# One step of a hybrid attention encoder on one core: GpSimd products in pieces, the first token loads, and the place of the per-layer inputs

## The chip, the cores and the metric

The kernel runs on one core of one Trainium2 chip, as one launch. The metric is device time in microseconds (us) of that launch. A core has five engines with queues of their own: TensorE (PE in the profile; its weight loads are shown apart as PEld), VectorE (DVE), ScalarE (ACT), GpSimd (POOL) and SyncE (SP), which issues all DMAs of this kernel in one order.

## The reference, cut to what matters

One layer over 2,048 prompt tokens and 32 sample tokens, width 1,024, all in float32. The parts that the change touches are the first norm and projection, the splits of every matrix product, and the per-layer inputs `p`.

```python
def rmsnorm(x, g, eps=EPS):
    y = x * lax.rsqrt(jnp.mean(x * x, axis=-1, keepdims=True) + eps)
    return y * g

z  = rmsnorm(hp, g_attn) @ w_in            # q, k, v of group A (4 heads, two maps) and group B (8 heads)
oa = diff_attn(qa, ka, va, t5_table, lam)  # softmax(map 1) - lam * softmax(map 2), chunk-causal
ob = band_attn(qb, kb, vb, band_table)     # each 64-token chunk sees itself and the 8 before
h  = hp + concat(rmsnorm(oa) * 0.8, rmsnorm(ob)) @ w_out
c  = rmsnorm(h, g_mlp)
h  = h + square(relu(c @ w_up)) @ w_down   # 1024 -> 4096 -> 1024
h  = h + sigmoid(h @ w_ple_gate) * (p @ w_ple_proj)      # p: 256 wide per token
y  = rmsnorm(h, g_final)
```

The keys and values of both groups are outputs too. The sample tokens attend to 128 cached keys besides their own.

## The kernel before

**Splitting.** TensorE works on a rounded 32-bit type (`F32R`). To keep float32 accuracy each operand is held as a high and a low half, and every product is three matmuls (`mm3`, L164 to L170: high by high at L168, high by low at L169, low by high at L170). The low half is "raw minus high". `split` (L146) makes both: the high half by a copy on ScalarE (L149) or VectorE (L151), the low half by a subtraction (L153) on GpSimd or VectorE. `wunit` (L155) loads a weight tile of 128 x 1,024 (`wr`, two buffers), and has it split on ScalarE and GpSimd into `wh` and `wl` (three buffers each). So each weight tile takes one GpSimd instruction of 1,024 columns.

**Stages.** `run` (L1074) writes the program in this order: constants and gains (`consts`); the norm and transpose of token blocks 0 and 1 (`prep`, four tiles of 128 tokens a block); the group A projections of these blocks (`proj`); the lambda, the relative biases and the per-layer inputs (`lam`, `biases`, `prep_p`); group A attention of the first half (`attn_a`), around which the scheduler lays the group B projections of blocks 0 to 2 and the norms of blocks 2 and 3; the cached keys and values (`caches`); the group B projection of block 3; group B attention (`attn_b`); then output projections, MLP (`mlp`), gate (`gate`) and final norm (`final`), laid around the rest of the attention. A block is 512 tokens; block 3 carries the 32 sample tokens as well.

**Who decides the order.** The tile framework takes the program order as a priority, and a scheduler that simulates the engines fixes, when the kernel is built, the order of the instructions on each engine. On the chip each engine runs its own list strictly in order, and so does SyncE with the DMAs. A tile name has a fixed number of buffers, handed out in program order: a later tile of the same tag can't be written before an earlier one has its buffer and has given it back.

**PSUM.** Two banks are tag `mm` (projections, MLP and most others), three are `s` (attention scores), two `tp` (attention transposes), one `o` (attention outputs).

**`prep`** (L297), for each tile: load `x`; square it on ScalarE with a row sum; `rsqrt` (L172) turns the sum `st` into the row factor, by Ln and Exp on ScalarE (L177, L178) and one Newton step in four small instructions (L179 to L182), on VectorE here; the factor is transposed and broadcast through PSUM (`rp`, `rb`); the tokens are transposed on TensorE (`xp`, L319), stored as `xT`, scaled on VectorE (L323) into `a32`, and split into `aH` (VectorE, L151) and `aL` (GpSimd). The PSUM tiles of the first two blocks come from the three banks `s`.

**`prep_p`** (L753): per block a load `pn`, eight transposes a block through PSUM tag `tp` (`ppt`), a split on ScalarE and VectorE into the tags `qh` and `ql` (two buffers each, shared with the projections), and the stores `pS`, which only `gate` reads, much later.

**`biases`** (L227) builds one row per head and spreads it to 128 rows in DRAM (`dba`, `dbb`); `attn_a` reads the table `ba` from it.

Of the kernel before, what the change touches and what calls it, by code (L numbers as in the profile page):

```python
# [76 lines left out]
JB = [(0, 1), (2, 3), (4, 5), (6, 7, 8)]  # L77
ONP = (28, 1, 6)
ONQ = (8, 1, 1)


def drain(gen):
    for _ in gen:
        pass
# [48 lines left out]
class Kern:  # L133
# [5 lines left out]
    def dma(self, dst, src):  # L139
# [3 lines left out]
            src = src.bitcast(F32)  # L143
        self.nc.sync.dma_start(dst, src)

    def split(self, hi, lo, raw, hi_eng="act", lo_eng="pool"):  # L146
        nc = self.nc
        if hi_eng == "act":
            nc.scalar.activation(hi, raw, AF.Copy)  # L149
        else:  # L150
            nc.vector.tensor_copy(hi, raw)  # L151
        eng = nc.gpsimd if lo_eng == "pool" else nc.vector
        eng.tensor_tensor(lo, raw, hi.bitcast(F32), op=ALU.subtract)  # L153

    def wunit(self, src, shape, hi_eng="act", lo_eng="pool"):  # L155
        nc = self.nc
# [15 lines left out]
    def rsqrt(self, pool, src, n, scale, eps, eng, tag="rs", np_=P, bufs=None):  # L172
        nc = self.nc
        v = pool.tile([P, n], F32, tag=tag + "v", bufs=bufs, name="rsv")[:np_]
        nc.scalar.activation(v, src, AF.Copy, scale=scale, bias=eps)
        y0 = pool.tile([P, n], F32, tag=tag + "y", bufs=bufs, name="rsy")[:np_]
        nc.scalar.activation(y0, v, AF.Ln)  # L177
        nc.scalar.activation(y0, y0, AF.Exp, scale=-0.5)  # L178
        eng.tensor_tensor(v, v, y0, op=ALU.mult)  # L179
        eng.tensor_tensor(v, v, y0, op=ALU.mult)  # L180
        eng.tensor_scalar(v, v, -0.5, 1.5, op0=ALU.mult, op1=ALU.add)
        eng.tensor_tensor(y0, y0, v, op=ALU.mult)  # L182
        return y0
# [7 lines left out]
    def consts(self, cp):  # L191
        nc, a = self.nc, self.a
        self.ident = cp.tile([P, P], F32, name="ident")
        make_identity(nc, self.ident)
        ones = cp.tile([P, P], F32, name="ones")
        nc.gpsimd.memset(ones, 1.0)
        self.ones = cp.tile([P, P], F32R, name="ones_r")
        nc.vector.tensor_copy(self.ones, ones)

        def cols(name, ap, k):  # L200
            t = cp.tile([P, k], F32, name=name)
            self.dma(t, ap.rearrange("(k p) -> p k", p=P))
            return t

        self.g_attn = cols("g_attn_s", a["g_attn"][0], 8)
        self.g_mlp = cols("g_mlp_s", a["g_mlp"][0], 8)
        self.g_b = cols("g_b_s", a["out_norm_b"][0], 4)
        self.g_sub = cols("g_sub_s", a["subln_g"][0], 1)
        nc.vector.tensor_scalar(self.g_sub, self.g_sub, 1.0 - LAM_INIT, None, op0=ALU.mult)
# [84 lines left out]
    def actpair(self):  # L294
        return [self.act.tile([P, 8, BLK], F32R, tag="act", name=n) for n in ("aH", "aL")]

    def prep(self, b, acts, pp, mm, tag):  # L297
        nc = self.nc
        aH, aL = acts[b]
        for c0, n in toks(b):  # L300
            t0 = 512 * b + c0
            x = pp.tile([P, D], F32, tag="x", name="x")
            self.dma(x[:n], self.xsrc(t0, n))
            a32 = pp.tile([P, 8, P], F32, tag="a32", name="a32")
            st = pp.tile([P, 1], F32, tag="st", name="st")
            nc.scalar.activation(
                a32[:n].rearrange("p a b -> p (a b)"), x[:n], AF.Square, accum_out=st[:n]
            )
            r = self.rsqrt(pp, st[:n], 1, 1.0 / D, EPS, nc.vector, "r1", n)
            rp = mm.tile([P, 512], F32, tag=tag, name="rp")  # L310
            nc.tensor.transpose(rp[:, :n], r.broadcast_to([n, P]), self.ident[:n, :n])
            rb = pp.tile([P, P], F32, tag="rb", name="rb")
            nc.scalar.activation(rb[:, :n], rp[:, :n], AF.Copy)
            xt = pp.tile([P, 8, P], F32, tag="xt", name="xt")
            for h in range(2):
                xp = mm.tile([P, 4, P], F32, tag=tag, name="xp")
                for k in range(4):
                    kk = 4 * h + k
                    nc.tensor.transpose(xp[:, k, :n], x[:n, kk * P : kk * P + P], self.ident[:n, :n])  # L319
                nc.scalar.activation(xt[:, 4 * h : 4 * h + 4, :n], xp[:, :, :n], AF.Copy)  # L320
                for k in range(4):
                    kk = 4 * h + k
                    nc.vector.scalar_tensor_tensor(  # L323
                        a32[:, kk, :n], xp[:, k, :n], self.g_attn[:, kk : kk + 1], rb[:, :n],
                        op0=ALU.mult, op1=ALU.mult,
                    )
            self.dma(self.xT[:, :, t0 : t0 + n], xt[:, :, :n])
            self.split(aH[:, :, c0 : c0 + n], aL[:, :, c0 : c0 + n], a32[:, :, :n], "dve", "pool")
            yield

    def ktok(self, b):
# [421 lines left out]
    def prep_p(self, sg, wk, ps):  # L753
        nc, a = self.nc, self.a
        for b in range(4):
            t0 = 512 * b
            n = BN[b]
            pn = wk.tile([P, 5, DPLE], F32, tag="pn", bufs=2, name="pn")
            self.dma(pn[:, :4], a["p_prompt"][0, 0, t0 : t0 + 512].rearrange("(i p) c -> p i c", p=P))
            if b == 3:  # L760
                self.dma(pn[:SS, 4], a["p_sample"][0, 0])
            for k in range(2):
                hi = sg.tile([P, BLK], F32R, tag="qh", bufs=2, name="pph")
                lo = sg.tile([P, BLK], F32R, tag="ql", bufs=2, name="ppl")
                pieces = [(0, 512)] + ([(512, SS)] if b == 3 else [])
                for c0, w in pieces:
                    tp = ps.tile([P, 512], F32, tag="tp", name="ppt")
                    for i in range(max(w // P, 1)):
                        m = min(w, P)
                        nc.tensor.transpose(  # L770
                            tp[:, P * i : P * i + m], pn[:m, c0 // P + i, P * k : P * k + P], self.ident[:m, :m]
                        )
# [12 lines left out]
    def onorm(self, b, wk, ps, tag, dst):  # L785
        nc = self.nc
        n, t0 = BN[b], 512 * b
        sq = wk.tile([P, BLK], F32, tag="acc", bufs=2, name="sqacc")[:, :n]
        for k in range(4, 8):
            raw = self.raw_o(wk, k, t0, n)  # L790
            if k == 4:
                nc.scalar.activation(sq, raw, AF.Square)
            else:
                nc.scalar.activation(raw, raw, AF.Square)
                nc.gpsimd.tensor_tensor(sq, sq, raw, op=ALU.add)
        yield from self.colnorm2(sq, b, 1.0 / 512, wk, ps, tag, dst, [])

    def oload(self, b, wk, up, out):
# [20 lines left out]
    def outproj(self, b, wk, oact, ps, acc):  # L819
# [5 lines left out]
        for d in range(8):  # L825
# [13 lines left out]
            if d == 0:  # L839
                nc.scalar.activation(sq, h, AF.Square)  # L840
            else:
                tmp = wk.tile([P, BLK], F32, tag="tmp", bufs=4, name="tmp")[:, :n]
                nc.scalar.activation(tmp, h, AF.Square)
                nc.gpsimd.tensor_tensor(sq, sq, tmp, op=ALU.add)
            self.dma(self.hS[:, d, t0 : t0 + n], h)
            yield

# [118 lines left out]
    def gate(self, b, h, up, act, md):  # L966
# [11 lines left out]
        for dq in range(2):  # L978
# [3 lines left out]
            for d4 in range(4):  # L982
                d = 4 * dq + d4
                wh, wl = self.wunit(Wg[:, P * d : P * d + P].rearrange("(k p) c -> p k c", p=P), [8, P])
                for s0, sn in SUBS[b]:
# [8 lines left out]
                    nc.vector.tensor_scalar(sm, pg, 0.0, None, op0=ALU.min)  # L994
                    nc.scalar.activation(sg, sg, AF.Exp, scale=-1.0)
                    nc.scalar.activation(sg, sg, AF.Ln, bias=1.0)
                    nc.gpsimd.tensor_tensor(sg, sm, sg, op=ALU.subtract)
                    nc.scalar.activation(sg, sg, AF.Exp)
                    pq = md.tile([P, 512], F32, tag="mm", name="pps")[:, :sn]
                    self.mm3(  # L1000
# [10 lines left out]
                    )  # L1011
                    nc.vector.tensor_tensor(sg, sg, pq, op=ALU.mult)
                    hv = h[:, d, s0 : s0 + sn]
                    nc.gpsimd.tensor_tensor(hv, hv, sg, op=ALU.add)
                yield

    def final(self, b, h, up, fk, mm, md=None):
# [56 lines left out]
    def run(self):  # L1074
        tc, nc, a = self.tc, self.nc, self.a
        with ExitStack() as top:
# [22 lines left out]
            with ExitStack() as x:  # L1099
                pp = opened(x, "pp0", 3, side="right")  # L1100
                acts = {b: self.actpair() for b in HALVES[0]}
                for b in HALVES[0]:
                    drain(self.prep(b, acts, pp, ps_s, "s"))
            ppx = ExitStack()
            pp = opened(ppx, "pp", 1)
            drain(self.proj(HALVES[0], 0, acts, sg, mm, Rings((ps_t, "tp"))))
            with ExitStack() as x:
                wk = opened(x, "setup", 1, side="right")
                self.lam(cp, wk)
                self.biases(wk, ps_t)  # L1110
                self.prep_p(sg, wk, ps_t)
            self.small = True
            mark = tc.tile_snap_priority()
            with ExitStack() as x:
# [20 lines left out]
            weave(self.proj((2,), 1, acts, sg, mm, tp), lifted(self.prep(3, acts, pp, mm, "mm")), 3)  # L1135
            ppx.close()
            self.caches(sg, tp)
            drain(self.proj((3,), 1, acts, sg, mm, tp))
            wqx = ExitStack()
            wq = opened(wqx, "wq", 1, side="right")  # L1140
# [143 lines left out]
```

## Time and profile before

| quantity | value |
|---|---|
| median of 3 runs | 3313.28 us (3307.74 to 3317.84) |
| the profiled execution: its own time | 3310.69 us |
| its span, first to last instruction | 3308.8 us |
| busy: TensorE, VectorE, ScalarE, GpSimd | 3096.1, 1669.4, 1698.4, 1468.8 us |
| GpSimd instructions | 1,083 |
| mean granted TensorE clock | 0.975 |

A row of the grouped view reads: line, engine, operation, output<-inputs, shape, count | busy us, mean ns of one | idle us of the engine just before them, and what ended it. A row of the windows view gives, for a stretch of the span, the busy us and the number of instructions of each engine, the granted TensorE clock (1.00 is full speed), the busy share of the DMA engines, and GB/s. A row of the waits reads: who waited, for whom, us in total, times, longest. A row of the timeline reads: start us, duration us, engine, line, operation, and in brackets the engine's idle time before it and what ended it. Adjacent instructions' rows overlap by some 0.05 us.

### The profile page before, as it was taken

What the parts mean: (1) busy time and instruction counts of PE and PEld (TensorE: products, weight loads), DVE (VectorE), ACT (ScalarE), POOL (GpSimd) and SP (SyncE); (2) the same over time, 40 slices, a digit from 0 to 9 for tenths busy, and PEclk for the clock granted to TensorE, in tenths of its full rate; (3) what the DMA queues carried; (4) which work ended last, traced back from release to release, by engine and by line L of the source; (5) the groups of instructions that cost most, each with busy time, mean ns of one, the idle gap of its engine ahead of it and who ended that gap; (6) DMA issues with size and microseconds to landing.
All of it is one profiled execution on the core that took longest, in us unless ns stands there. A gap on an engine that the chain in (4) does not pass through costs nothing. (4 is left out here: it accounts for less than half of the span.)

```text
span 3308.8 us, 50118 instructions
## 1 busy us (share of the span) xinstructions
PE 3096.1 (94%) x17881; PEld 2710.5 (82%) x17881; DVE 1669.4 (50%) x3952; ACT 1698.4 (51%) x3717; POOL 1468.8 (44%) x1083
## 2 busy tenths in 40 slices
PE   6988989999989999999899999989889999999998
PEld 6877778889977888777777877877779999999987
DVE  6117777454555545476765656656442232223335
ACT  4226666566665766666665656654442222222245
POOL 4335654432334433444544444565753333333365
PEclk9999899999999999999999999999999999999999
DMA  7488777686788654545655345347631111111123
GB/s 232 159 252 244 205 217 205 204 247 195 215 235 215 180 145 134 155 132 138 200 136 136 112 132 144 116 146 226 178 105 52 45 46 50 46 45 45 53 86 101
DMA packets 519073, 488.93 MB, mean 148 GB/s; under 512 B 37884, under 2 KB 414016, under 8 KB 518824
## 3 DMA queue, kind: packets, MB, share of 16 engines
q1 hardware_dynamic: 518824, 485.73, 50.8%
q8 instruction: 142, 2.33, 0.3%
q14 instruction: 107, 0.88, 0.1%
HBM read 379.06 MB, written 110.49 MB: 148 GB/s over the span
## 5 line engine op out<-in xcount | busy, mean ns | idle before, releaser
L153 POOL TENSOR_TENSOR wl<-wr,wh 128x1024 fp32r<-128x1024 f32 x338 | 820.0, 2427 | 1026.3 <-ACT wh L149 983.4
L949 DVE TENSOR_TENSOR h<-h,dps 128x512 f32<-128x512 f32 (+1 forms) x640 | 373.1, 585 | 584.6 <-PE dps L170 572.2
L149 ACT ACTIVATE wh<-wr 128x1024 fp32r<-128x1024 f32 x338 | 356.9, 1056 | 563.9 <-PE dps L169 278.4
L168 PE MATMUL dps<-uh,wh 128*128 128x512 f32 (+1 forms) x1280 | 459.7, 359 | 22.0 <-DVE h L949 16.7
L168 PE MATMUL ups<-cH,wh 128*128 128x512 f32 (+1 forms) x1280 | 452.0, 353 | 8.2 <-ACT relu L914 8.0
L170 PE MATMUL dps<-uh,wl 128*128 128x512 f32 (+1 forms) x1280 | 451.7, 353 | 0.0
L169 PE MATMUL ups<-cL,wh 128*128 128x512 f32 (+1 forms) x1280 | 451.5, 353 | 0.0
L169 PE MATMUL dps<-ul,wh 128*128 128x512 f32 (+1 forms) x1280 | 451.4, 353 | 0.0
L170 PE MATMUL ups<-cH,wl 128*128 128x512 f32 (+1 forms) x1280 | 451.0, 352 | 0.0
L168 PEld LDWEIGHTS dps<-uh,wh 128*128 128x128 f32 x1280 | 242.8, 190 | 57.0 <-DVE h L949 22.8
L168 PEld LDWEIGHTS ups<-cH,wh 128*128 128x128 f32 x1280 | 241.4, 189 | 40.9 <-ACT relu L914 8.6
L170 PEld LDWEIGHTS dps<-uh,wl 128*128 128x128 f32 x1280 | 241.7, 189 | 33.0
L169 PEld LDWEIGHTS ups<-cL,wh 128*128 128x128 f32 x1280 | 241.9, 189 | 31.1 <-DVE cL L153 0.4
L170 PEld LDWEIGHTS ups<-cH,wl 128*128 128x128 f32 x1280 | 241.7, 189 | 30.1
L153 POOL TENSOR_TENSOR ul<-relu,uh 128x272 fp32r<-128x272 f32 (+1 forms) x160 | 174.9, 1093 | 205.2 <-ACT uh L149 203.8
L169 PEld LDWEIGHTS dps<-ul,wh 128*128 128x128 f32 x1280 | 242.4, 189 | 26.3
L168 PE MATMUL qps<-aH,wh 128*128 128x512 f32 (+1 forms) x640 | 231.5, 362 | 6.8 <-ACT wh L149 3.4
L545 PE MATMUL s<-ka,q 128*128 128x256 f32 (+4 forms) x784 | 192.7, 348 | 40.8 <-issue 15.7
L169 PE MATMUL qps<-aL,wh 128*128 128x512 f32 (+1 forms) x640 | 229.8, 359 | 0.0
L170 PE MATMUL qps<-aH,wl 128*128 128x512 f32 (+1 forms) x640 | 229.3, 358 | 0.0
L559 ACT ACTIVATE e<-s,nm 128x512 f32<-128x512 f32 (+3 forms) x256 | 155.1, 610 | 94.7 <-DVE nm L551 70.9
L545 PEld LDWEIGHTS s<-ka,q 128*128 128x128 f32 (+1 forms) x784 | 135.7, 195 | 66.4 <-issue 27.9
(217 smaller groups left out, 7056.9 us busy)
## 6 DMA issues: line engine op xcount, KB each, us to landing
wr<-w_up SPq DMA_DIRECT2D x96, 512.0 KB, 4.2
wr<-w_down SPq DMA_DIRECT2D x96, 512.0 KB, 3.7
wr<-w_in SPq DMA_DIRECT2D x74, 512.0 KB, 5.2
q<-qS SPq DMA_DIRECT2D x256, 128.0 KB, 4.3
v<-vSa SPq DMA_DIRECT2D x64, 512.0 KB, 3.8
ka<-kS SPq DMA_DIRECT2D x32, 512.0 KB, 7.9
wr<-w_out SPq DMA_DIRECT2D x32, 512.0 KB, 5.0
wr<-w_ple_gate SPq DMA_DIRECT2D x32, 512.0 KB, 4.4
```

What stands on the lines that cost most here:

```text
L149: nc.scalar.activation(hi, raw, AF.Copy)
L153: eng.tensor_tensor(lo, raw, hi.bitcast(F32), op=ALU.subtract)
L168: nc.tensor.matmul(ps, lh, rh, start=start and i == 0, stop=False)
L169: nc.tensor.matmul(ps, lh, rl, start=False, stop=False)
L170: nc.tensor.matmul(ps, ll, rh, start=False, stop=stop and i == n - 1)
L545: nc.tensor.matmul(s, q[:, m, hl, P * qi : P * qi + nr], kt[:, m, k0 : k0 + n], start=hl == 0, stop=hl == 1)
L559: nc.scalar.activation(dst, src, AF.Exp, bias=nmx, accum_out=z[:nr, m, bi : bi + 1])
L949: nc.vector.tensor_tensor(hv, hv, ps, op=ALU.add)
```

## The change

Four things change.

1. `pool_tt` is new. Six places that had one GpSimd `tensor_tensor` now call it, the low half of `split` among them, and it cuts the columns into pieces of at most 256. A weight tile takes four instructions in place of one, a 512-column tile two. The products of `rsqrt` on GpSimd and the squares of `attn_a` have at most 256 columns and stay as they are. The built program has 2,520 GpSimd instructions where it had 1,088.
2. `rsqrt` for a single column writes its Newton step with three `tensor_scalar` instructions, whose factors come as per-row scalars, in place of three `tensor_tensor` and one `tensor_scalar`.
3. The four gain vectors are loaded by `gains`, which `prep` calls after the load of the first token tile. In `prep` the copy to `aH` goes from VectorE to ScalarE, and for the first two blocks the PSUM tiles alternate between the tags `s` (three banks) and `tp` (two).
4. `prep_p` goes from behind `biases` to behind `caches`, in a pool of its own, and its transposes take the tag `mm`.

```diff
+PW = 256
+    def pool_tt(self, out, a, b, op):
+        nc = self.nc
+        if len(out.shape) == 2:
+            n = out.shape[1]
+            m = -(-n // PW)
+            for i in range(m):
+                sl = slice(n * i // m, n * (i + 1) // m)
+                nc.gpsimd.tensor_tensor(out[:, sl], a[:, sl], b[:, sl], op=op)
+            return
+        k, n = out.shape[1:]
+        if n > PW:
+            for i in range(k):
+                self.pool_tt(out[:, i], a[:, i], b[:, i], op)
+            return
+        s = PW // n
+        for i in range(0, k, s):
+            sl = slice(i, min(i + s, k))
+            nc.gpsimd.tensor_tensor(out[:, sl], a[:, sl], b[:, sl], op=op)
...
-        eng = nc.gpsimd if lo_eng == "pool" else nc.vector
-        eng.tensor_tensor(lo, raw, hi.bitcast(F32), op=ALU.subtract)
+        if lo_eng == "pool":
+            self.pool_tt(lo, raw, hi.bitcast(F32), ALU.subtract)
+        else:
+            nc.vector.tensor_tensor(lo, raw, hi.bitcast(F32), op=ALU.subtract)
...
+        if n == 1:
+            eng.tensor_scalar(v, v, y0, y0, op0=ALU.mult, op1=ALU.mult)
+            eng.tensor_scalar(v, v, -0.5, 1.5, op0=ALU.mult, op1=ALU.add)
+            eng.tensor_scalar(y0, y0, v, None, op0=ALU.mult)
+            return y0
...
-    def prep(self, b, acts, pp, mm, tag):
+    def prep(self, b, acts, pp, mm, tag, first=None):
...
             self.dma(x[:n], self.xsrc(t0, n))
+            if first is not None:
+                first()
+                first = None
...
-            self.split(aH[:, :, c0 : c0 + n], aL[:, :, c0 : c0 + n], a32[:, :, :n], "dve", "pool")
+            self.split(aH[:, :, c0 : c0 + n], aL[:, :, c0 : c0 + n], a32[:, :, :n], "act", "pool")
...
-                    tp = ps.tile([P, 512], F32, tag="tp", name="ppt")
+                    tp = ps.tile([P, 512], F32, tag="mm", name="ppt")
...
-                nc.gpsimd.tensor_tensor(sq, sq, raw, op=ALU.add)
+                self.pool_tt(sq, sq, raw, ALU.add)
...
-                    drain(self.prep(b, acts, pp, ps_s, "s"))
+                    ring = Rings((ps_s, "s"), (ps_t, "tp"))
+                    drain(self.prep(b, acts, pp, ring, "s", (lambda: self.gains(cp)) if b == 0 else None))
...
                 self.biases(wk, ps_t)
-                self.prep_p(sg, wk, ps_t)
...
             self.caches(sg, tp)
+            with ExitStack() as x:
+                self.prep_p(sg, opened(x, "pn", 1), mm)
             drain(self.proj((3,), 1, acts, sg, mm, tp))
```

The other three `tensor_tensor` lines (in `outproj` and twice in `gate`) change as the one shown.

More of the change, by code (lines that the diff above doesn't have):

```diff
@@ L198, in consts, with gains @@
         nc.vector.tensor_copy(self.ones, ones)
+    def gains(self, cp):
+        nc, a = self.nc, self.a
         def cols(name, ap, k):
@@ L843, in outproj @@
                 nc.scalar.activation(tmp, h, AF.Square)
-                nc.gpsimd.tensor_tensor(sq, sq, tmp, op=ALU.add)
+                self.pool_tt(sq, sq, tmp, ALU.add)
             self.dma(self.hS[:, d, t0 : t0 + n], h)
@@ L996, in gate @@
                     nc.scalar.activation(sg, sg, AF.Ln, bias=1.0)
-                    nc.gpsimd.tensor_tensor(sg, sm, sg, op=ALU.subtract)
+                    self.pool_tt(sg, sm, sg, ALU.subtract)
                     nc.scalar.activation(sg, sg, AF.Exp)
@@ L1013, in gate @@
                     hv = h[:, d, s0 : s0 + sn]
-                    nc.gpsimd.tensor_tensor(hv, hv, sg, op=ALU.add)
+                    self.pool_tt(hv, hv, sg, ALU.add)
                 yield
```

## The prediction

> **What bounds the kernel now.** I read the windows of the span (3308.8 us) first, then what TensorE waited for inside the weak windows, then the timeline at those waits.
>
> ```profile
> 0.00:60.00 60.00, 36.06 (x250) 33.53 (x251) 46.42 (x117) 30.90 (x80) 31.22 (x24) 0.97 0.77 234
> 60.00:190.00 130.00, 126.99 (x674) 107.26 (x673) 23.95 (x34) 29.12 (x47) 48.19 (x32) 0.99 0.52 172
> 190.00:250.00 60.00, 50.49 (x287) 42.66 (x285) 10.37 (x21) 15.50 (x27) 23.10 (x16) 0.89 0.95 285
> 250.00:700.00 450.00, 398.85 (x2549) 359.70 (x2548) 304.15 (x888) 282.20 (x781) 234.66 (x223) 0.94 0.77 219
> ...
> 1400.00:2200.00 800.00, 753.80 (x3836) 632.16 (x3835) 515.11 (x1077) 494.54 (x1150) 378.09 (x276) 0.99 0.49 136
> 2200.00:2500.00 300.00, 268.41 (x1457) 231.07 (x1456) 155.12 (x213) 136.65 (x250) 181.63 (x108) 0.95 0.55 170
> 2500.00:3200.00 700.00, 700.00 (x4289) 632.56 (x4288) 200.60 (x375) 204.28 (x345) 249.65 (x162) 1.00 0.16 49
> ```
>
> TensorE is the bound, and from 2500 to 3200 us it never rests: nothing in this change can help there. What can be won is its idle time elsewhere (the stretch less the first figure: 23.9 us at the start, 9.5 before the first attention, 51.2 in the first attention stage, 46.2 and 31.6 later), and a reduced clock beside it: a granted mean of 0.94 over 450 us is some 27 us, 0.89 over 60 us 6.6 us, 0.95 over 300 us 15 us. In the first of these stages and in the attention VectorE is the busiest engine after it.
>
> ```profile
> PE s L545 <- issue: 7.2, 2, 4.0
> PE tpp L617 <- DVE e L582: 6.6, 6, 2.3
> PE rp L311 <- DVE rsy L182: 5.2, 3, 3.1
> ...
> PE s L545 <- DVE nm L554: 2.1, 2, 1.4
> ...
> PE xp L319 <- DVE ql L405: 2.0, 1, 2.0
> ...
> PE ss L642 <- DVE sh L151: 1.7, 1, 1.7
> ```
>
> These are TensorE's waits in 250 to 700 us: 17.6 us of them in 13 waits ended with VectorE. The timeline tells why VectorE was late.
>
> ```profile
> 12.89 4.65 POOL L153 TENSOR_TENSOR wl<-wr,wh 128x1024 fp32r<-128x1024 f32 x2 [11.39 <-ACT rsy L178]
> 12.93 2.32 DVE L179 TENSOR_TENSOR rsv<-rsv,rsy 128x1 f32<-128x1 f32 x1 [0.70 <-ACT rsy L178]
> 15.29 2.27 DVE L180 TENSOR_TENSOR rsv<-rsv,rsy 128x1 f32<-128x1 f32 x1
> ...
> 17.69 1.13 DVE L323 SCALAR_TENSOR_TENSOR a<-xp,g_attn_s,rb 128x128 f32<-128x128 f32 x4
> ...
> 303.63 2.53 POOL L153 TENSOR_TENSOR wl<-wr,wh 128x1024 fp32r<-128x1024 f32 x1
> 304.08 2.23 DVE L151 CAST sh<-sq 128x256 fp32r<-128x256 f32 x1
> 306.45 0.55 PE L642 MATMUL ss<-sh,ones_r 128*128 128x256 f32 x1 [1.74 <-DVE sh L151]
> ```
>
> A product of one column takes 2.32 us, and ends when GpSimd's first subtraction does; the second ends with the second. At 304 us a cast does the same, and TensorE waits for it. So a VectorE instruction with two tensors, or a plain cast, that meets a running GpSimd product waits for its end. It is not so with VectorE's other work: the four scalings at 17.69 read `xp` from PSUM and take 0.28 us apiece.
>
> **The change part by part.** *Pieces on GpSimd.* Their price on GpSimd itself first.
>
> ```profile
> L153 POOL TENSOR_TENSOR wl<-wr,wh 128x1024 fp32r<-128x1024 f32 x338 | 820.0, 2427 | 1026.3 <-ACT wh L149 983.4 <-ACT rsy L178 11.4 <-ACT pH L624 9.7
> L153 POOL TENSOR_TENSOR vhl<-vraw,vhl 128x256 fp32r<-128x256 f32 x64 | 48.0, 750 | 92.1 <-DVE vhl L151 74.6 <-DVE stb L713 8.6 <-DVE nm L557 3.8
> ```
>
> ```profile
> PE ops L170 <- POOL wl L153: 1.2, 2, 0.9
> ```
>
> Four pieces at 0.750 make 3.00 us in place of 2.427: +0.57 a tile, some 200 us over 338 weight tiles and 16 token tiles, so GpSimd goes from 44% busy to about half. It is hidden by the 1,026 us in which GpSimd waits for the next tile. Where that cover is gone TensorE waits for `wl`, as the last row shows twice among the waits of 2200 to 2500 us; 0.57 more at these two and at two that I allow for more is +2 us (bounds 0 and +15, if the gates and output projections there, GpSimd 61% busy, lose it at 26 tiles).
>
> *What VectorE gets.* A blocked instruction waits for the rest of a piece, 0.75 us at most, not of 2.4. I take two thirds off the waits that end with VectorE. In 250 to 700 us that is 12 of the 17.6 us. The reduced clock follows the gaps: 12 of 51.2 idle us carries 6 of the 27 us, and an earlier chain also eases the two waits called issue, 2 of 7.2. Together -20 us (bounds -5, if something else is late at once, and -45, if it takes half of the 78 us lost there).
>
> In 1400 to 2200 us and 2200 to 2500 us:
>
> ```profile
> PE dps L168 <- DVE h L949: 16.7, 14, 3.1
> ...
> PE ups L168 <- ACT relu L914: 8.0, 1, 8.0
> ...
> PE gps L168 <- DVE sm L994: 4.0, 3, 3.1
> PE ops L168 <- DVE hd L838: 3.6, 3, 1.9
> ```
>
> The MLP's additions `h` read PSUM and are late only because they queue behind attention work on VectorE; I take a third, -6 us (0 to -15). In the second stretch -9 (0 to -18): two thirds of the 7.6 us that end with VectorE, and half of the 8.0, whose queue starts in the norms on VectorE.
>
> *The row factor in other instructions.* Rows of small VectorE instructions:
>
> ```profile
> L181 DVE TENSOR_SCALAR rsv<-rsv 128x1 f32<-128x1 f32 x28 | 4.2, 150 | 0.7
> L572 DVE TENSOR_SCALAR c<-c,rz 128x3 f32<-128x3 f32 x16 | 9.3, 583 | 0.3
> ```
>
> The one-column form is never late, 28 of them at 0.150 us. With three columns and a factor from a tensor it is late at times. The new instructions have one column, so I count them as free of the wait. The Trainium skill (SBUF — State Buffer, Who interferes with whom) says that VectorE and GpSimd share one pair of ports, held for a whole instruction by whoever starts first, and that `tensor_scalar`, too, can take the pair: the trace agrees at three columns, at one not. By that rule the row factors would still wait, 0.75 us twice for the first tile: a sum 1.5 us higher.
>
> *The start.*
>
> ```profile
> 0.74 0.47 SPq L144 DMA_DIRECT2D g_attn_s<-g_attn  x1
> ...
> 3.05 1.38 SPq L144 DMA_DIRECT2D x<-x_prompt  x3
> ```
>
> The first tile is issued at 0.74 and not 3.05: -2.3 us. The scaling at 17.69 no longer stands behind 4.6 us of blocked products: -4.3. Three GpSimd tiles ahead of the first low halves cost +1.7. The copy to `aH` on ScalarE (30.9 of 60 us busy) is covered; uncovered it would cost about 1 us a tile. Five PSUM banks let the transposes run ahead: -1. Together -6 (bounds -2.3, as the DMA engines are 0.77 busy there and may set the pace, and -15 of the 23.9 idle us). From 60 to 190 us TensorE is 127.0 of 130 us busy, so this carries through.
>
> *`prep_p`, where it was.*
>
> ```profile
> PE ppt L770 <- DMA pn<-p_prompt: 6.9, 1, 6.9
> ```
>
> ```profile
> 191.81 1.03 PE L246 MATMUL pb<-ob,tb 128*8 128x256 f32 x4
> 193.23 0.28 PE L168 MATMUL vps<-wh,aH 128*128 128x256 f32 x1
> 193.35 0.28 PE L169 MATMUL vps<-wl,aH 128*128 128x256 f32 x1
> ...
> 199.98 5.56 SPq L144 DMA_DIRECT2D dbb<-rb  x8
> 236.54 0.57 SPq L144 DMA_DIRECT2D ba<-dba  x1
> 240.60 3.04 SPq L144 DMA_DIRECT2D q<-qS  x3
> ```
>
> The 6.9 us wait goes, and the 16 stores and 3 loads on SP's list between 205.5 and 240 us. In the new lists the attention's first loads stand right behind the eight `dbb`, and on TensorE 141 value matmuls (0.12 us each by the two rows) follow the last `pb`, then 14 score matmuls with nothing between. Matmuls end at 192.8 + 141 x 0.12 = 209.7. The loads need 7.1 us of issue (236.54 to 243.64), to 212.6, and must land through full DMA engines (0.95), about 5 us more (the landing row below has 4.2 to 8.4): TensorE waits some 8 us, and the first scores run without filler. 6.9 out, 8 in, the stage's clock as now: 0 (bounds -9 and +8).
>
> *`prep_p`, where it goes.* Its transposes now take `mm` banks in program order, so the projection of block 3 behind it can't fill in. The new TensorE list has 24 transposes in one run, and between the cached keys and the sixteenth band score matmul no projection at all.
>
> ```profile
> L770 PE MATMUL ppt<-ident,pn x34: 243/272/445, 194.8 to 237.4; 128*128 128x128 f32 x32, 32*128 32x32 f32 x2
> ```
>
> ```profile
> DMA to landing us min/median/max: 4.2/6.2/8.4
> ```
>
> The second row belongs to what writes `ppl` and to its stores. Two buffers must go out before the tile after next is written: (4.2 + 1.3 of copying) / 2 = 2.75 us for each of eight tiles, 22 us, in which TensorE has about 10 us of transposes and attention: +12 (bounds 0, and +41 if it takes the 42.6 us of before with hardly any cover). I take the least landing, as DMA share there is 0.77, not 0.95.
>
> The sum: +2 - 20 - 6 - 9 - 6 + 0 + 12 = -27 us. The profiled execution took 3310.7 us; less 27 is 3283.7. The median of the runs lies 2.6 us above, so I forecast 3286 us (-0.8%). The row-factor rule would make it 3288.
>
> **The rivals.** *Slower:* the new place of `prep_p` decides. For: its stores stand on SP's list between the first loads of the band attention, 13 issues of 0.6 us ahead of one store that a buffer waits for. Against: those loads are early in the list. Price: +41 for the ring, +7 of clock as in 190 to 250 us, +8 for the issues, in place of +12: +17, 3328 us, or 3330 on the median's footing. It decides once it costs over 39 us. *The pieces do nothing:* GpSimd's adjacent pieces leave no room for VectorE. Against it stands the pair at 12.89, between whose instructions VectorE got in. Then only -4 at the start stays, +2 and +12: 3321 us, 3323. *More than I take:* VectorE's lateness stands behind the waits that name ScalarE, issue and `h` too. For: every rise of VectorE's busy share goes with TensorE's losses. Then -40, -15, -18, -8 at the start, -4 before the attention, +2, +10: -73, 3238 us, 3240.
>
> **How the numbers follow.** Forecast 0.60, slower rival 0.13, pieces without effect 0.08, more than taken 0.19. About 0.3% (10 us) is what a measurement tells from no change. The forecast is faster in 0.55 and within 0.3% in 0.05; the large case is faster; the pieces' case lies at its edge, half within and half slower; the slow case is slower in 0.10 and within in 0.03. So faster 0.74, same 0.12, slower 0.14. The bounds of the costs, as roots of summed squares, lie 32 us below and 37 above; they are extremes, so I take half as the forecast's own range, 3270 to 3305. The range reaches to the cases on both sides, 3238 to 3332.
>
> **What would show it.** Right: VectorE's longest one-column products and casts under 0.9 us; TensorE above 403 us busy in its first attention stage of 450, with a clock above 0.95; the first `x` issued at 0.7 us; GpSimd busy 1,600 to 1,700 us. A stretch of some 20 us with transposes `ppt` and little else would be the +12. Wrong: casts still at 2 us; a wait over 15 us at `ppt` or `sb`; a clock below 0.97 over the whole.

## The result, and the profile after

| | before | after |
|---|---|---|
| median of the runs shown with the result | 3313.89 us (3307.74 to 3317.84) | 3282.61 us (3278.72 to 3286.44) |
| profiled execution: own time, span, clock | 3310.69, 3308.8, 0.975 | 3278.72, 3276.9, 0.972 |
| TensorE busy | 3096.1 us | 3095.0 us |
| VectorE busy | 1669.4 us | 1539.6 us |
| GpSimd busy | 1468.8 us | 1701.7 us |

The ratio is 0.9911, with an interval of 0.9894 to 0.9928: 31 us less, where the forecast, 3286, was 28 less. TensorE's busy time is the same, so the gain is idle time: 212.7 us before (span less busy), 181.9 after.

The windows of the changed kernel; the columns are, as before, busy time (and instructions) of TensorE, its weight loads, VectorE, ScalarE and GpSimd, then granted clock, DMA share and GB/s. Line numbers are those of the kernel that a row is from, so `split` and the rest stand some 20 to 33 lines lower here (the pieces of GpSimd are L154 and L164, the copies L169 and L171):

```profile
0.00:60.00 60.00, 39.91 (x266) 37.33 (x267) 31.26 (x100) 37.24 (x88) 36.26 (x58) 0.94 0.76 236
60.00:190.00 130.00, 128.80 (x692) 107.54 (x691) 18.07 (x36) 29.39 (x48) 54.36 (x76) 1.00 0.52 174
190.00:250.00 60.00, 48.89 (x282) 42.86 (x281) 22.12 (x90) 25.25 (x75) 25.11 (x37) 0.86 0.89 240
250.00:700.00 450.00, 405.49 (x2604) 367.04 (x2603) 276.16 (x915) 312.69 (x819) 259.87 (x393) 0.92 0.82 238
...
1400.00:2200.00 800.00, 762.03 (x3810) 637.45 (x3809) 470.70 (x1016) 487.86 (x1099) 459.89 (x651) 0.98 0.49 139
2200.00:2500.00 300.00, 274.51 (x1538) 240.24 (x1537) 131.69 (x195) 129.81 (x241) 203.19 (x281) 0.95 0.49 153
```

Idle time falls by 5.7 us up to 190 us, by 6.6 in 250 to 700, by 8.2 in 1400 to 2200 and by 6.1 in 2200 to 2500. (Later windows hold the same stretch of time, not quite the same work, as the two kernels drift apart by up to 31 us.) The first attention stage has two faces, which its mean hides. Finer windows of the changed kernel:

```profile
250.00:530.00 280.00, 260.69 (x1535) 230.07 (x1534) 195.37 (x612) 203.03 (x558) 199.18 (x284) 0.95 0.80 232
530.00:560.00 30.00, 13.27 (x64) 10.31 (x63) 7.65 (x18) 7.44 (x16) 8.71 (x16) 0.59 0.85 253
560.00:700.00 140.00, 131.54 (x1008) 126.66 (x1008) 73.14 (x286) 102.22 (x246) 51.98 (x94) 0.95 0.85 246
```

and of the kernel before:

```profile
250.00:530.00 280.00, 240.77 (x1399) 210.39 (x1398) 213.37 (x619) 179.11 (x520) 162.93 (x145) 0.92 0.80 222
530.00:560.00 30.00, 28.52 (x167) 24.79 (x165) 20.96 (x50) 19.02 (x46) 13.87 (x12) 0.97 0.65 187
```

Up to 530 us the changed kernel wins 20 us of idle time and 0.03 of clock. Then come 30 us in which TensorE works 13 and is granted 0.59. What it waited for in this stage, from the list of waits of the changed kernel in 250 to 700 us:

```profile
PE ppt L803 <- DVE ppl L807: 6.3, 4, 3.4
...
PE sb L737 <- DMA q<-qS: 5.2, 1, 5.2
PE tpp L650 <- DVE e L615: 3.9, 5, 1.7
...
PE ppt L803 <- DMA pn<-p_prompt: 3.2, 1, 3.2
PE ss L675 <- DVE sh L171: 2.8, 2, 1.6
```

The stretch is `prep_p` at its new place: transposes that wait for a buffer (`ppl`) or for `pn`, then the band attention's first `sb` (at 558.1 us), whose `q` is issued from 550.6 us on, behind seven of `prep_p`'s stores and three of its loads. The old waits for VectorE are smaller: `tpp` 6.6 before, 3.9 now.

One thing at the start was not in the forecast. The timeline of the changed kernel:

```profile
21.79 2.81 POOL L164 TENSOR_TENSOR aL<-a,aH 128x256 fp32r<-128x256 f32 x4
...
24.13 6.09 DVE L171 CAST vhl<-vraw 128x256 fp32r<-128x256 f32 x1 [2.70 <-ACT vraw L394]
24.56 2.79 POOL L164 TENSOR_TENSOR wl<-wr,wh 128x256 fp32r<-128x256 f32 x4
...
27.31 2.77 POOL L164 TENSOR_TENSOR aL<-a,aH 128x256 fp32r<-128x256 f32 x4
30.15 0.26 DVE L202 TENSOR_SCALAR rsv<-rsv,rsy 128x1 f32<-128x1 f32 x1
...
30.90 0.47 PE L344 MATMUL rp<-ident,rsy 128*128 128x128 f32 x1 [5.19 <-DVE rsy L204]
```

A cast that takes 0.3 us alone begins while GpSimd works and ends after nine pieces, when GpSimd has nothing left to do. It did not get in between adjacent pieces. TensorE waits 5.2 us for the row factor queued behind it. The same happens to one `cL`:

```profile
L175 DVE TENSOR_TENSOR cL<-tmp,cH x16: 671/920/10759, 1040.3 to 2393.2; 128x512 fp32r<-128x512 f32 x12, 128x544 fp32r<-128x544 f32 x4
```

(durations in ns, least, median and greatest): 10.8 us through 17 pieces, at 2374 us. These are two of some 215 VectorE instructions that were more than 0.3 us late; the others got in at the first or second end of a piece.

### The profile page after: what moved, and what is told of

It is laid out like the page before. It is cut to its first block, busy times and chain, and to the rows that moved or that the text cites. A ratio compares the mean times of both kernels' runs of the same rounds, so it can differ in the third digit from the quotient of the medians.

```text
span 3276.9 us, 51580 instructions
## 1 busy us (share of the span) xinstructions
PE 3095.0 (94%) x17881; PEld 2712.0 (83%) x17881; DVE 1539.6 (47%) x3906; ACT 1711.3 (52%) x3734; POOL 1701.7 (52%) x2515
## 4 chain that ended last, share of the span: by engine, by line
PE 53%; DMA 5%; DVE 5%; ACT 1%; issue 1%; POOL 1%; SPq 1%; DVEq 0%; POOLq 0%; ACTq 0%
PE ups L190 7%; PE dps L190 7%; PE ups L191 7%; PE ups L192 7%; PE dps L191 6%; PE dps L192 6%; PE s L578 2%; PE gps L190 2%; PE gps L191 2%; PE gps L192 2%; DMA ka<-kS 1%; PE tpp L650 1%; DVE e L615 1%; PE o L665 1%; PE o L666 1%
## 5 line engine op out<-in xcount | busy, mean ns | idle before, releaser
L164 POOL TENSOR_TENSOR wl<-wr,wh 128x256 fp32r<-128x256 f32 x936 | 691.4, 770 | 499.1 <-ACT wh L169 431.3
L169 ACT ACTIVATE wh<-wr 128x1024 fp32r<-128x1024 f32 x338 | 357.3, 1057 | 577.3 <-PE dps L191 299.0
L154 POOL TENSOR_TENSOR wl<-wr,wh 128x256 fp32r<-128x256 f32 x416 | 301.5, 755 | 403.4 <-ACT wh L169 402.3
L154 POOL TENSOR_TENSOR ul<-relu,uh 128x136 fp32r<-128x136 f32 (+1 forms) x320 | 198.0, 640 | 170.3 <-ACT uh L169 169.1
L584 DVE TENSOR_REDUCE nm<-s 128x1 f32<-128x512 f32 (+3 forms) x256 | 147.7, 588 | 96.1 <-PE s L578 95.2
```

Of the source, the lines that this page charges most:

```text
L154: nc.gpsimd.tensor_tensor(out[:, sl], a[:, sl], b[:, sl], op=op)
L164: nc.gpsimd.tensor_tensor(out[:, sl], a[:, sl], b[:, sl], op=op)
L584: nc.vector.tensor_reduce(nmx, s, axis=AX.X, op=ALU.max, negate=True)
```

## The experiments

Ratios are to the kernel before, from runs on the same chip. The order of all instructions is planned anew whenever one changes, so an edit also changes the lists of the engines; where that matters, the text says by how much: lines taken out plus lines put in, between TensorE's 17,881 instructions of one trace and of the other, told apart by tile names and shapes. The recorded expectations count this in another way.

| | edit | ratio (interval) | VectorE busy | GpSimd busy |
|---|---|---|---|---|
| e1 | pieces whole again | 1.0055 (1.0038 to 1.0071) | 1642 | 1464 |
| e2 | pieces alone | 0.9893 (0.9874 to 0.9911) | 1553 | 1711 |
| e3 | `prep_p` at its old place | 0.9869 (0.9844 to 0.9894) | 1537 | 1703 |
| e4 | old row factor | 0.9935 (0.9914 to 0.9956) | 1548 | 1705 |
| e5 | old start | 0.9935 (0.9914 to 0.9957) | 1548 | 1717 |
| e6 | 512 columns | 1.0056 (1.0038 to 1.0074) | 1588 | 1537 |
| e7 | 128 columns | 1.0112 (1.0094 to 1.0130) | 1521 | 2012 |
| e8 | `prep_p` spread | 0.9873 (0.9858 to 0.9887) | 1528 | 1702 |
| e9 | uneven pieces | 0.9897 (0.9870 to 0.9924) | 1544 | 1714 |
| e10 | as e9 | 0.9908 (0.9887 to 0.9930) | 1539 | 1713 |
| e11 | e8, 17 of the 68 `vhl` casts on ScalarE | 0.9827 (0.9803 to 0.9851) | 1529 | 1707 |
| e12 | factor in four one-column forms | 0.9948 (0.9928 to 0.9968) | 1541 | 1707 |

### The pieces: e1 and e2

```diff
     def pool_tt(self, out, a, b, op):
...
+        self.nc.gpsimd.tensor_tensor(out, a, b, op=op)
```

> The changed kernel with GpSimd's products whole again, everything else kept. Theory (pieces free VectorE, and this is most of the gain): the forecast's terms for it were -20, -6, -9 and +2, so 33 us are lost: about 3316 us, ratio to the kernel before 1.000, VectorE's casts and e products up to 2.1 us late again, GpSimd busy some 1,500 us. Rival (pieces do nothing, the gain is the start and the place of prep_p): about 3283 us, ratio 0.991.

> The kernel before with GpSimd's products in pieces of 256 columns, nothing else changed. Theory: -33 us by the same terms: about 3281 us, ratio 0.990, as fast as the whole change, because the other parts add up to +6. Rival (pieces do nothing): 3314 us, ratio 1.000. A middle result, with e1 in the middle too, would say that the parts overlap: row factors and pieces both take away the same blocked products.

Without pieces the rest of the change is slower than the kernel before, 1.0055: 48 us above the changed kernel (0.0144 of 3311). Pieces alone give 0.9893, 35 us. So the gain is the pieces'. The other parts together cost 18 us without pieces; beside pieces the 6 us that they seem to cost (0.9911 against 0.9893) are less than what a change of order, with little else, brings in e4 and e12 (below). That the pieces do nothing is excluded.

How they do it is less plain. TensorE's waits that end with VectorE, in us, summed over its list of waits with `prep_p`'s own left out; the last column has e3, e4, e5 and e8 to e12:

| | before | e1 (whole) | e6 (512) | e7 (128) | after (256) | e2 (256) | the eight others with 256 |
|---|---|---|---|---|---|---|---|
| 250 to 700 us | 23.8 | 22.0 | 27.5 | 24.4 | 11.6 | 13.1 | 8.8 to 20.2 |
| 1400 to 2200 us | 20.9 | 22.7 | 17.2 | 25.5 | 19.9 | 13.2 | 12.1 to 22.4 |
| whole span | 86.8 | 80.5 | 76.0 | 82.6 | 64.0 | 73.6 | 58.3 to 69.1 |

In 250 to 700 us the changed kernel and e2 have half the waits of both kernels with whole products, but e4 and e8, in pieces of 256 too, have 20.2 and 19.8, and e8 is among the fast ones. Neither stage tells the two kinds apart. The whole span does: 58 to 74 us in all ten kernels with 256 columns, 76 to 87 in the four without. Of the 44.5 us of idle time between e1 (3325.0 - 3098.6 = 226.4) and the changed kernel (181.9), the waits put down to VectorE give 16 (87.1 to 70.8 over the span, `prep_p`'s included) and those put down to DMA 18 (63.7 to 46.1). The 44.5 are more than VectorE's lateness explains by itself.

### The length: e6 and e7

```diff
-PW = 256
+PW = 512
```

and 128 for e7.

> The changed kernel with PW = 512. One piece costs 0.19 + 512 x 0.00218 = 1.31 us by the two rows of before (128x256 0.750, 128x1024 2.427). Theory (the loss goes with the length that a blocked instruction waits for): (1.31 - 0.75) / (2.43 - 0.75) of the 48 us between e1 and the changed kernel, 16 us: 3299 us, ratio 0.9955. Rival (only the longest waits count, and half is short enough): 3283 us, 0.991, with GpSimd some 100 us less busy.

> The changed kernel with PW = 128: a piece at 0.47 us by the same line, eight of them 3.76 us a weight tile, GpSimd some 270 us busier (60% of the span). Theory (length decides): (0.75 - 0.47) / 1.68 of 48 us, 8 us less: 3275 us, ratio 0.9885, if GpSimd stays hidden. Rival 1 (GpSimd's cover is gone at 2200 to 2500 us, where it is 75% busy in the changed kernel): waits for wl of 15 us or more there, 3290 us or more, 0.993. Rival 2 (short pieces starve VectorE more often than twice): single VectorE instructions of 5 us and more.

VectorE's busy time, which holds its lateness, falls with the length: 1642, 1588, 1540, 1521 us for whole products, 512, 256 and 128. The time does not follow: 1.0055, 1.0056, 0.9911, 1.0112. Both expectations of the theory fail.

For 512 TensorE's idle time does follow: 203 us, between 226 with whole products and 182 with 256. But its busy time is 3,118 us, 19 more than in e1. The windows of e6 name one place:

```profile
530.00:560.00 30.00, 21.33 (x90) 16.76 (x88) 10.60 (x41) 13.75 (x34) 10.53 (x16) 0.74 0.78 221
560.00:640.00 80.00, 62.24 (x290) 48.89 (x290) 47.59 (x196) 60.31 (x152) 2.34 (x16) 0.71 0.76 221
```

and the last 80 us in the changed kernel:

```profile
560.00:640.00 80.00, 76.83 (x583) 72.75 (x583) 44.33 (x180) 61.52 (x160) 25.52 (x46) 0.94 0.87 259
```

In these 80 us of e6 GpSimd has 2.3 us of work: no weight tile is split, so no projection runs beside the band attention, and the granted clock is 0.71. That is an order of the list, not a wait for a piece. The 30 us ahead of them are better in e6, though (21.3 us of work against 13.3), so over the 110 us it loses 6.5 us of work (83.6 against 90.1) and 0.12 of clock (0.72 against 0.84). How much of e6's 48 us this carries was not isolated.

For 128 GpSimd is near full in one stage. The window and the waits of e7:

```profile
2200.00:2500.00 300.00, 257.38 (x1330) 217.83 (x1329) 121.84 (x179) 129.29 (x234) 250.47 (x554) 0.93 0.50 157
```

```profile
PE ups L190 <- ACT relu L947: 9.0, 1, 9.0
PE ops L190 <- DVE hd L871: 7.2, 3, 4.0
PE gps L192 <- POOL wl L164: 6.6, 2, 5.9
```

GpSimd works 250 of 300 us, and TensorE has 17 us less work done than in the changed kernel, of the 67 (0.0201 of 3311) that e7 loses against it. The 15 us of waits for `wl` that the first rival wanted are 6.6; the other rows name VectorE and ScalarE, so that a full GpSimd is behind them is likely, not shown. The second rival holds beside it:

```profile
L920 DVE TENSOR_TENSOR sqacc<-sqacc,r x10: 430/696/7347, 940.0 to 2373.9; 128x512 f32<-128x512 f32 x6, 128x272 f32<-128x272 f32 x4
```

```profile
L171 DVE CAST vhl<-vraw x68: 272/294/7371, 25.0 to 798.8; 128x256 fp32r<-128x256 f32 x64, 32x256 fp32r<-32x256 f32 x4
```

A product and a cast of 7.3 us: behind shorter pieces VectorE is passed over more often, with five instructions held up by 11 pieces or more, against none or one in each kernel with 256.

### Wait or order: e9, e10

```diff
-                sl = slice(n * i // m, n * (i + 1) // m)
+                sl = slice(0, n - 16 * (m - 1)) if i == 0 else slice(n - 16 * (m - i), n - 16 * (m - 1 - i))
```

> The changed kernel with its pieces uneven: for a weight tile one of 976 columns and three of 16, in place of four of 256; as many instructions and columns, and nearly the same lists of instructions on every engine (TensorE's differ in 564 lines of 16,000). Theory (what pieces give is the shorter wait of VectorE): the waits are 2.3 us again, and most of the 48 us between e1 and the changed kernel comes back: 3315 to 3330 us, ratio 1.000 to 1.0055. Rival (what pieces give is another order of the lists, since e1 and e6 have quite other lists): 3283 us, ratio 0.991, though VectorE waits as long as in e1.

> The same lists as e9, instruction by instruction, with weight tiles in pieces of 496, 496, 16 and 16 columns; one of 496 costs 0.19 + 496 x 0.00218 = 1.27 us. Theory (loss in proportion to the length of the wait): between the changed kernel and e9, about a third of the way, 3298 us, ratio 0.995. Rival 1 (e6 was slow by its length): as slow as e9 or e1. Rival 2 (e6 was slow by its order alone, the band attention without a projection beside it at 550 to 650 us): 3283 to 3290 us.

The edit reached a part of what it aimed at. Of the 338 weight tiles, 234 have three dimensions with short rows (128x4x256 or 128x8x128), which the lower branch of `pool_tt` cuts: they kept their four even pieces. The other 104 have two rows of 512 columns, the down projection's among them, and each row became 496 and 16, as other tiles of 512 columns did; 544 columns became 512, 16 and 16. These 104 all lie behind 1000 us. No tile has four pieces in one row, so e10 is the same program as e9, and the two are a repeat of each other (0.9897 and 0.9908).

What they show is narrower than was asked, but the comparison is clean: TensorE's list differs from the changed kernel's in 126 lines, and VectorE's waits, passed-over instructions aside, reach 1.1 us in place of some 0.6. In 1400 to 2200 us, where nearly half of these tiles are, TensorE works 762.7 us in both, and 762.0 in the changed kernel. There the longer wait costs nothing. Whether the 234 other tiles, every one ahead of 1000 us among them, act by the wait or by the order that four instructions bring about was not tried, and stays open.

### `prep_p`: e3 and e8

```diff
                 self.biases(wk, ps_t)
+                self.prep_p(sg, wk, ps_t)
...
-            with ExitStack() as x:
-                self.prep_p(sg, opened(x, "pn", 1), mm)
```

> The changed kernel with prep_p behind the biases again (banks ps_t, pool of the setup). Theory: the new place costs 12 us net and the old one 0 beside it, so this is faster: about 3271 us, ratio 0.987; TensorE's stretch of ppt and little else at 534 to 558 us is gone, and a wait of ppt for pn is back at about 206 us. Rival 1 (the two places cost the same): 3283 us, 0.991. Rival 2 (the old wait of 6.9 us and its 16 stores come back in full and the new place is hidden): 3290 us or more, 0.993.

0.9869, 14 us better than the changed kernel: the theory's number, and both rivals fall. TensorE idles 30.8 us in 250 to 700 us, where the changed kernel idles 44.5. The window of e3:

```profile
530.00:560.00 30.00, 28.61 (x233) 27.43 (x232) 15.50 (x41) 16.34 (x39) 19.62 (x27) 1.00 0.55 172
```

The stretch is gone, and `ppt` waits 6.2 us for `pn` at 213 us again, as it did before.

```diff
-                self.prep_p(sg, opened(x, "pn", 1), mm)
-            drain(self.proj((3,), 1, acts, sg, mm, tp))
+                side = self.prep_p(sg, opened(x, "pn", 1), mm)
+                weave(self.proj((3,), 1, acts, sg, mm, tp), side, 1)
```

> The changed kernel with prep_p's eight tiles spread between the parts of the projection of block 3, in place of ahead of them; banks mm as in the changed kernel. Theory (the ring of two buffers and TensorE's list without a projection make the 12 to 14 us): both are covered by projection matmuls, 14 us less: 3268 us, ratio 0.987, like e3. Rival (the stores and loads on SP's list delay the band attention's first q, 5.2 us in the changed kernel, and projection weights beside them): half of it or nothing, 3276 to 3283 us. If it beats e3, the new place is the better one, once the tiles are spread.

With a `yield` after each tile's stores, `prep_p` runs between the steps of the projection: 0.9873, as e3. TensorE works 28.5 of the 30 us, and of the stretch's waits only `sb` for `q` is left, 3.7 us at 568 us. So the new place is as good as the old one once projection matmuls lie between the tiles. That the block of transposes, on banks that the projection needs, is what cost the 14 us fits both runs, but e8 does not show it cleanly: over 250 to 700 us it idles as long as the changed kernel (43.8 against 44.5 us), as it loses around the 30 us what it wins in them. Its gain shows in the granted clock of this stage, 0.95 against 0.92, and in 9 us less busy time over the span.

### The row factor: e4 and e12

```diff
-        if n == 1:
...
-            return y0
```

> The changed kernel with the row factor by two-tensor products again (pieces stay). Theory (one-column form free of the wait, a blocked product now waits for one piece only): at the start two products at up to 0.75 us each for the tiles that meet GpSimd, about 2 us more: 3285 us, ratio 0.9915, rows of rsv at up to 0.9 us. Rival (the form decides the start): 4 us or more, 3287 us or more, with rows at 2 us. Second rival (the new form waits as well, so nothing changes): 3283 us, with rows of rsv as in the changed kernel.

```diff
-            eng.tensor_scalar(v, v, y0, y0, op0=ALU.mult, op1=ALU.mult)
+            eng.tensor_scalar(v, v, y0, None, op0=ALU.mult)
+            eng.tensor_scalar(v, v, y0, None, op0=ALU.mult)
```

> The changed kernel with the row factor in four one-column tensor_scalar instructions, as many as e4 has, but none of two tensors. Theory A (e4's 8 us are blocked two-tensor products): as fast as the changed kernel, 3283 us, ratio 0.991. Theory B (e4's 8 us are its other lists of instructions, as its losses lie at 250 to 700 and 1400 to 2200 us and not at the start): anywhere between the changed kernel and e4 or beyond, 0.988 to 0.995, with rows of rsv of 0.15 to 0.28 us all the same.

The rows of the factor in the changed kernel:

```profile
L202 DVE TENSOR_SCALAR rsv<-rsv,rsy x29: 252/271/276, 6.6 to 3233.0; 128x1 f32<-128x1 f32 x28, 32x1 f32<-32x1 f32 x1
L203 DVE TENSOR_SCALAR rsv<-rsv x29: 134/153/155, 6.9 to 3233.3; 128x1 f32<-128x1 f32 x28, 32x1 f32<-32x1 f32 x1
L204 DVE TENSOR_SCALAR rsy<-rsy,rsv x29: 195/214/215, 7.1 to 3233.5; 128x1 f32<-128x1 f32 x28, 32x1 f32<-32x1 f32 x1
```

and in e4:

```profile
L201 DVE TENSOR_TENSOR rsv<-rsv,rsy x30: 142/297/749, 6.6 to 3279.6; 128x1 f32<-128x1 f32 x28, 32x1 f32<-32x1 f32 x1, 128x5 f32<-128x5 f32 x1
L202 DVE TENSOR_TENSOR rsv<-rsv,rsy x30: 144/257/733, 6.8 to 3279.8; 128x1 f32<-128x1 f32 x28, 32x1 f32<-32x1 f32 x1, 128x5 f32<-128x5 f32 x1
```

The two-tensor product is late by up to 0.6 us, the one-column form with a factor never: its greatest is 5 ns above its median of 271. The mechanism is as expected. The time is not its doing: e12 has no two-tensor product in these factors, and is as slow as e4 (0.9948 and 0.9935). Theory B holds. At the start e4 is even ahead of the changed kernel: its last `pb` matmul ends at 183.8 us against 187.4, as no cast is passed over. Their losses lie in 250 to 700 us (TensorE busy 398.7 and 397.5 us, against 405.5), where eight of the 29 factors are made, and in 1400 to 2200 us (754.4 and 753.6 against 762.0), where none is. The two share a fourth instruction and, nearly, one order: TensorE's lists differ from the changed kernel's in 3,460 and 3,612 lines, from each other in 986. So some 8 to 12 us come and go with an edit that only adds a small instruction and changes the order, and no part of the change that is worth less can be read from one kernel.

### The start: e5 and e11

```diff
-                    drain(self.prep(b, acts, pp, ring, "s", (lambda: self.gains(cp)) if b == 0 else None))
+                    drain(self.prep(b, acts, pp, ps_s, "s"))
...
-            self.split(aH[:, :, c0 : c0 + n], aL[:, :, c0 : c0 + n], a32[:, :, :n], "act", "pool")
+            self.split(aH[:, :, c0 : c0 + n], aL[:, :, c0 : c0 + n], a32[:, :, :n], "dve", "pool")
```

> The changed kernel with the start undone: the gains loaded ahead of the first token tile, transposes in the three banks ps_s alone, aH copied on VectorE. Theory: -2.3 for the load, -1 for the banks and part of the -4.3 for VectorE's work come back: 4 to 6 us, 3287 to 3289 us, ratio 0.9925; TensorE's first 60 us lose 4 us or more against the changed kernel's 20.1 idle. Rival (the DMA engines or the chain of one tile set the pace): only the 2.3 us of the first issue, 3285 us, 0.9918.

The whole came out as the theory said, 0.9935, but not by the start: the loss lies where e4's does (396.6 us of TensorE's work in 250 to 700, 752.9 in 1400 to 2200). The end of the first stage is the end of the last `pb` matmul: 192.8 us before, 187.4 in the changed kernel, and 183.5 in e5 with the old start. TensorE has 40.7 us of work in e5's first 60 us at a clock of 1.00, against 39.9 at 0.94. The first row factor reaches TensorE at 11.2 us in place of 7.3, and by the fourth tile e5 is ahead (26.7 against 30.9 us), because no cast is passed over. e1 (new start, whole products, no cast passed over) ends the stage at 184.3. One starved cast outweighs what the new start brings beside the new factor. The two parts overlap: with pieces but the old start and the old factor (e2) the stage ends at 190.9 us, so either new part alone takes 7 us off it (e4 and e5, with `prep_p` moved as well), and both without a starved cast (e11, below) 9.

```diff
-                    self.split(hl[:n, :, 0], hl[:n, :, 1], r3[:n], "dve", "pool")
+                    self.split(hl[:n, :, 0], hl[:n, :, 1], r3[:n], "act" if grp == 0 and c == 0 else "dve", "pool")
```

> e8 with the high halves of the first value columns of the first group (vhl) copied on ScalarE and not on VectorE. In e8, as in the changed kernel, VectorE's first such copy took 6.0 us at 24 us behind nine GpSimd pieces in a row, and TensorE waited 5.1 us for the row factor behind it. Theory (one starved instruction costs TensorE its wait): TensorE's wait at 31 us goes, 5 us less: 3261 us, ratio 0.9855. Rival (the next instruction of VectorE is starved in its place, or the time is given back by 190 to 250 us, where DMA sets the pace): 3266 us, 0.987.

TensorE's waits for row factors in the first 60 us, in e8:

```profile
PE rp L344 <- DVE rsy L204: 15.4, 6, 5.1
```

and in e11:

```profile
PE rp L344 <- DVE rsy L204: 7.5, 4, 4.3
```

The 5.1 us wait is gone and the stage ends at 181.8 us, 5.4 before e8: the theory's price for one starved instruction. The ratio falls by 0.0046, 15 us, to a median of 3249.47; of the other 10 or so, 7 show in 250 to 700 us (413.2 us of TensorE's work against 406.2) under lists that differ in 3,216 lines, and are not explained. e11 is the fastest of all: 0.9827, with the changed kernel at 0.9911.

## Why the prediction was right, and where it was not

The sum was right within 3.4 us of the median, and some of its terms by their own mechanism. That it came so near is in part luck: single terms missed by more than that, and in e4 and e12 a new order with one small instruction more moves the time by two or three times as much.

- *What bounds the kernel.* Held: all of the gain is idle time of TensorE, and from 2500 to 3200 us nothing moved.
- *Pieces on GpSimd, +2.* 1,702 us of work, just over the 1,600 to 1,700 forecast. TensorE's waits for GpSimd fell from 5.9 to 3.1 us over the span, so the cover held. In e7, with GpSimd 83% busy in 2200 to 2500 us, that stage loses 17 us.
- *VectorE freed, -20 in 250 to 700 us.* The 12 us of waits came (23.8 to 11.6, and 13.1 in e2; the 17.6 in 13 waits of the prediction were the largest rows, the whole list has 23.8 in 21), and up to 530 us the clock rose with them, 0.92 to 0.95. Other kernels with the same pieces show up to 20.2 there, so these 12 are not the pieces' alone. As a total for all stages, 33 us, the pieces' price was near the 35 of e2 and short of the 48 of e1. The step that failed is "a blocked instruction waits for the rest of a piece, 0.75 us at most": in two places it waited for 9 and for 17 pieces. The rival that gave the pieces no effect had named this, adjacent pieces that leave no room, and was right about these two alone. And length does not set the time, as e6 shows; the reason given for the 33 us is at best a part of it. One piece of the prediction's evidence does not bear on it either: the four scalings at 17.69 us, said not to be held up by GpSimd, ran while GpSimd was idle (its products end at 17.54 us, the next starts at 20.72); the eight from 20.67 us on do show it, at 0.27 us each beside a product.
- *-6 and -9 later.* Idle time fell by 8.2 and 6.1. In 1400 to 2200 us the additions `h` fell from 16.7 to 7.8 us, more than the third taken, but waits for `sm`, on the same engine, took 10.8 us that were not in that stage's list before; all waits for ScalarE there fell from 8.0 to 1.9. In 2200 to 2500 us the one wait of 8.0 for `relu`, of which the prediction took half, came out at 4.4; but the waits that end with VectorE fell only from 11.5 to 10.3, as one starved `cL` alone made 4.3. Right size, in part by other rows.
- *The start, -6.* 5.5 us by the last `pb`, by luck. The load first is worth 3.6 us to the first tile (10.9 to 7.3), and beside the new factor nothing by the fourth; the 4.3 for blocked products was paid back as 5.2 for one starved cast. With e2, e4, e5 and e11 the start and the factor are worth 7 us each and 9 together, not the sum of separate terms.
- *The row factor.* Free of the wait, as counted: 29 of 29 at 0.252 to 0.276 us. The Trainium skill (SBUF — State Buffer, Who interferes with whom) counts `tensor_scalar` among the operations that can take the pair of ports shared with GpSimd, when its operands meet certain conditions. The prediction's 1.5 us took it that one column meets them; this trace shows no such wait.
- *`prep_p`, 0 and +12.* The wait for the first `q` came, 7.8 and 1.6 us against 8, and the old 6.9 went. The new place cost 16.7 us of idle time in 30, and e3 puts the net at 14. The ring (`ppl`, 6.3 us) was named rightly; the missing projection fits e8, with the limit said there. That the band's first `q` waits too (5.2 us) was in the slower rival; it came, but small.
- *The signs.* Of the signs of being right, the first `x` at 0.7 us, TensorE above 403 us in its first attention stage (405.5) and the stretch of `ppt` came. VectorE's longest casts under 0.9 us and a clock above 0.95 in that stage did not: 6.1 us, and 0.92.

## What to carry to other kernels

Cutting one engine's long products into pieces can be worth a per cent by itself where another engine's instructions wait for their end. The length has to be tried: here 256 columns won, and 512 and 128 gave nothing or worse, for reasons that the runs show only in part. A block of short work that takes the same buffers as the filler behind it can leave the bound engine idle for half of the stretch (16.7 of 30 us here); spread between the filler's steps it cost nothing that shows. And where a planner reorders everything on every edit, effects of a third of a per cent belong to no edit until a kernel with the same lists shows them.

## What the runs showed of the hardware

Between adjacent GpSimd pieces VectorE mostly gets its turn, and then the next piece waits for it: in the timeline of the changed kernel

```profile
285.73 2.99 POOL L164 TENSOR_TENSOR wl<-wr,wh 128x256 fp32r<-128x256 f32 x4 [0.55 <-ACT wh L169]
...
287.16 0.97 DVE L171 CAST qh<-kr 128x512 fp32r<-128x512 f32 x1
```

four pieces take 2.99 us with VectorE's work between, against 2.79 in the undisturbed row at 24.56 us. But it is not granted every time: with the same kinds of instruction it was passed over for 8 to 18 pieces in a row, with 256 columns each time until GpSimd had an empty moment, and more often with pieces of 128 columns. What decides it, these traces do not show. Pieces of `wl` of 128, 256 and 512 columns took 0.480, 0.766 and 1.334 us on average, near the line through 256 and 1024 columns that the expectations used.
